# The recurrence chain of a hybrid RWKV-7 / MLA layer: one PSUM bank per head pair, the output's state product moved beside U, a full-width identity product, and the state copied on by ScalarE

## Chip, cores and metric

The kernel runs on one core of one Trainium2 chip. The metric is the device time of one execution in microseconds (us). Three executions were timed, and one more was profiled; the profile gives times in us from the start of its span.

## The reference

One decoder layer over a sequence of 1024 tokens of width 1024. A modulated RMSNorm feeds one input projection. Its columns go to two groups: an RWKV-7 recurrence (8 heads of 64) and a latent attention (8 heads). Both are gated, concatenated and mapped back by an output projection; a final RMSNorm closes. The part that matters here is the recurrence:

```python
def step(state, inp):
    r_t, w_t, k_t, v_t, kk_t, a_t = inp
    sa = jnp.einsum('bhvk,bhk->bhv', state, kk_t)
    state = (state * w_t[:, :, None, :]
             - sa[..., None] * (kk_t * a_t)[:, :, None, :]
             + v_t[..., None] * k_t[:, :, None, :])
    y = jnp.einsum('bhvk,bhk->bhv', state, r_t)
    return state, y
```

It is a serial scan over the tokens with a 64x64 state for every head. All of it is float32.

## The kernel before

**Stages.** First the modulated, normalised and transposed input is made, in two parts whose sum is the float32 value (`hTh`, `hTl`). Then comes a long stage in which the input projection, cut into tiles of 128 output columns, runs as filler of TensorE (`mm3`, lines 164 to 166: three matmuls of 128x512 for each tile and slice of the contraction), while the recurrence is prepared and carried out between these matmuls. Then the attention follows, and last the output projection.

**The recurrence in chunks.** It is done in chunks of `C` = 64 tokens. A unit is four heads (two pairs, `a` = 0, 1; the two heads of a pair, `s` = 0, 1, lie on partitions 0 to 63 and 64 to 127, `rows[s]`) over 256 tokens, that is four chunks. There are eight units: four for heads 0 to 3, then four for heads 4 to 7. `prep`, `products`, `invert`, `fetch`, `tmat`, `turn_kb` and `turn_v` make a unit's matrices beforehand: `GA` (masked products, its columns 0 to C for the chain's first step and C to 2C for the output), `TT` (the inverse of a triangular matrix), `KB` (keys, for the state's update), `rq` (decayed receptance) and `eL` (the decay over the chunk). `ST` holds for each chunk, on one half of the partitions, the values and on the other half first the incoming state and then U.

**The chain.** `chain(un, nxt)` is the serial part. For each of the four chunks `i` it has three steps, with a `yield` after each, so that other work is emitted between them:

- step 1: four products `GA` x `ST` (L694, contraction over 128 rows, 64 columns), and one copy of the result to `X` by ScalarE (L697);
- step 2: four products `TT` x `X` (L701, 64 rows, 64 columns), and two scaled copies by ScalarE which write -U into `ST` (L703, L704);
- step 3: the next state. For each pair two products with a 64x64 identity add the old state `Sv` (L709), and two products `KB` x `ST` (L712, 128 rows) add to it. ScalarE multiplies by `eL` four times into the next chunk's `ST` (L720, 64 partitions each) and two times into `Sn` (L722, 128 partitions). Then the chunk's output `Y`: for each pair two products `rq` x `Sv` (L725, 64 rows) and two products `GA` x `ST` (L728, 128 rows).

The first chunk of heads 0 to 3 and of heads 4 to 7 has no old state; the last chunk of each has no next state. In PSUM (eight banks) the tile `rc` with the three results is one bank, `Y` of a unit is another, and the tags `mm`, `rp` and `rt` have two each. `post` (L739) copies a unit's `Y` to SBUF in one copy of 128x512 and normalises it.

**What sets the order.** The loop at the end of the code goes through stages `n` = 0 to 10 and steps `j` within each. At every second `j` it resumes the chain of unit `n` - 2; at fixed `j` it calls the parts of the units that are being prepared or finished; and at each `j` it emits `RATE[n]` slices of the filler. The instructions of each engine are then put in order by a planner that goes by priority (the order of emission) and by when it reckons operands to be ready; `quick` raises the priority of the chain's ScalarE instructions by 20 places (100 in the last units). On the chip each engine runs its instructions in that order. The dependencies in PSUM are kept by the framework.

Of the kernel before, what the change touches and what calls it, by code (L numbers as in the profile page):

```python
# [17 lines left out]
F32 = mybir.dt.float32  # L18
# [9 lines left out]
P = 128  # L28
# [3 lines left out]
HALF = 512  # L32
# [3 lines left out]
C = 64  # L36
# [50 lines left out]
def hymba_kernel(ctx: ExitStack, tc: tile.TileContext, x, pos, cols, cst, winit, w_ada, b_gate, w_in, w_lora, w0,  # L87
# [157 lines left out]
    with ExitStack() as s0:  # L245
# [62 lines left out]
        for i in range(4, 8):  # L308
            load_x(i)
        ws.append(load_w(GROUP[2][0], P, st, 3, st))  # L310
        acc = [[(psM if m == 0 else psA).tile([P, HALF], F32, tag=t, name=f"acc{m}{h}", bufs=1 if m == 1 else 2)
                for h, t in enumerate(tags)] for m, tags in enumerate((("mm", "mm"), ("rc", "ry"), ("rt", "rt")))]
# [365 lines left out]
    def chain(un, nxt):  # L678
# [8 lines left out]
        ps = psA.tile([P, 3, 2, C], F32, tag="rc", name="rc", bufs=1)  # L687
        Y = un["Y"] = psA.tile([P, 8, C], F32, tag="ry", name="Y", bufs=1)
        for i in range(4):
            last = i == 3 and nxt is None  # L690
            cc = [a * 4 + i for a in range(2)]
            for a in range(2):
                for s in range(2):
                    T.matmul(ps[rows[s], 0, a, :], lhsT=GA[s][a][:, i, 0:C], rhs=ST[:, cc[a], s, :], start=True, stop=True)  # L694
            X = ch.tile([P, 2, C], F32, tag="X", name="X", bufs=2)
            with quick(un):
                A.copy(X[:], ps[:, 0])  # L697
            yield
            for a in range(2):
                for s in range(2):  # L700
                    T.matmul(ps[rows[s], 1, a, :], lhsT=TT[rows[s], cc[a], :], rhs=X[rows[s], a, :], start=True, stop=True)  # L701
            with quick(un):
                A.mul(ST[lo, i:8:4, 0, :], ps[lo, 1], -1.0)  # L703
                A.mul(ST[hi, i:8:4, 1, :], ps[hi, 1], -1.0)  # L704
            yield
            Sn = None if last else ch.tile([P, 2, C], F32, tag="S", name="S", bufs=2)
            for a in range(0 if last else 2):
                for s in range(2 if Sv else 0):
                    T.matmul(ps[rows[s], 2, a, :], lhsT=ident[rows[s], rows[s]], rhs=Sv[rows[s], a, :],  # L709
                             start=True, stop=False)  # L710
                for s in range(2):
                    T.matmul(ps[rows[s], 2, a, :], lhsT=KB[:, s, cc[a], :], rhs=ST[:, cc[a], s, :],  # L712
                             start=Sv is None, stop=True)
            if not last:

                dst, n = (ST, i + 1) if i < 3 else (nxt["ST"], 0)
                with quick(un):
                    for a in range(2):
                        for s in range(2):
                            A.mul(dst[rows[s], a * 4 + n, s, :], ps[rows[s], 2, a, :], eL[rows[s], cc[a]:cc[a] + 1])  # L720
                    for a in range(2):
                        A.mul(Sn[:, a], ps[:, 2, a], eL[:, cc[a]:cc[a] + 1])  # L722
            for a in range(2):
                for s in range(2 if Sv else 0):
                    T.matmul(Y[rows[s], cc[a], :], lhsT=rq[rows[s], cc[a], 1, :], rhs=Sv[rows[s], a, :],  # L725
                             start=True, stop=False)
                for s in range(2):
                    T.matmul(Y[rows[s], cc[a], :], lhsT=GA[s][a][:, i, C:2 * C], rhs=ST[:, cc[a], s, :],  # L728
                             start=Sv is None, stop=True)
            Sv = Sn  # L730
            if i == 3 and nxt:
                nxt["S"] = Sv
            yield

    def post(un):
# [3 lines left out]
        A.copy(ys[:], Y[:])  # L739
# [270 lines left out]

    turned, la = [], latents()
# [374 lines left out]
```

## Time and profile before

| what | value |
|---|---|
| three timed executions | 925.86, 933.34, 2558.89 us; median 933.34 us |
| the profiled execution's own time | 920.99 us |
| its span in the profile | 918.8 us, 16567 instructions |
| TensorE (PE) busy with matmuls | 835.3 us, 91% of the span |
| VectorE (DVE) busy | 575.3 us, 63% |
| ScalarE (ACT) busy | 476.5 us, 52% |
| GpSimd (POOL) busy | 296.2 us, 32% |

PE is the matmul part of TensorE and PEld its weight loads. A float32 matmul stands in the trace as two records, so that four products of a step show as "x8". A row of the timeline gives a group's start, its length, engine, line, tiles and the shape: "128*64 128x64" is contraction rows by output columns of the array, then the moving operand. The ends of matmuls are modelled and overlap with the next ones, so how long a group holds the engine is read from the start of the group to the start of the next. In the windows, PEclk is the mean of the clock that TensorE was granted, 1.00 being full speed.

### The profile page before, as it was taken

Reading aid. Unit: us, or ns where it says so; the run is one execution under the profiler, and the core shown is the slowest. Engines: PE = TensorE matmul, PEld = TensorE weight load, DVE = VectorE, ACT = ScalarE, POOL = GpSimd, SP = SyncE. Lnnn points to the kernel's source line nnn. Section 1 sums busy time; section 2 is a strip of 40 time slices with the busy share of each in tenths; the row PEclk is TensorE's granted clock in tenths of the full one; section 3 lists DMA queues with packets and bytes.
Section 4 is the critical chain, followed back from the end, with each engine's and each line's share of the span. In section 5 each row is a group of like instructions: output and inputs, shape, how many; then the busy total and the mean of one; then the engine's idle time right before and its main releaser. Section 6 shows DMA issues by size and latency. Waiting matters only on the chain.

```text
span 918.8 us, 16567 instructions
## 1 busy us (share of the span) xinstructions
PE 835.3 (91%) x5812; PEld 641.2 (70%) x5812; DVE 575.3 (63%) x1462; ACT 476.5 (52%) x1112; POOL 296.2 (32%) x351
## 2 busy tenths in 40 slices
PE   1798997999999999898899999997799998989996
PEld 0586785776777777566667767765678777868885
DVE  5795349378495654955757366247778788765443
ACT  2655332444644636346245464554778888873311
POOL 1311423131232323423133122223436454454400
PEclk9999999999999999998999999999999999999998
DMA  8764433333435324435333254157102031017233
GB/s 253 247 194 153 140 110 115 95 105 88 134 118 150 118 69 135 121 69 165 118 99 104 65 151 139 49 172 203 55 18 70 21 110 59 1 56 239 85 126 126
DMA packets 131714, 106.66 MB, mean 116 GB/s; under 512 B 40616, under 2 KB 108464, under 8 KB 131632
## 3 DMA queue, kind: packets, MB, share of 16 engines
q1 hardware_dynamic: 130672, 102.46, 37.5%
q0 software_dynamic: 960, 3.15, 1.5%
q8 instruction: 46, 0.75, 0.3%
q14 instruction: 36, 0.29, 0.1%
HBM read 76.46 MB, written 29.10 MB: 115 GB/s over the span
## 4 chain that ended last, share of the span: by engine, by line
PE 66%; DVE 13%; ACT 9%; issue 4%; DMA 4%; POOL 2%; SPq 1%; POOLq 0%; DVEq 0%; ACTq 0%
PE mm L164 10%; PE mm L165 8%; PE mm L166 8%; PE po L1160 3%; PE po L1162 3%; PE po L1161 3%; PE gps L577 3%; ACT pr L1087 2%; DVE wtmp L625 2%; DVE W L627 2%; PE tp L1098 2%; ACT PTh L1107 1%; PE rc L712 1%; PE rc L694 1%; PE Y L728 1%
## 5 line engine op out<-in xcount | busy, mean ns | idle before, releaser
L164 PE MATMUL mm<-hTh,whi 128*128 128x512 f32 (+1 forms) x384 | 167.2, 435 | 3.1 <-DVE wtmp L625 2.3
L166 PE MATMUL mm<-hTh,wlo 128*128 128x512 f32 (+1 forms) x384 | 156.9, 409 | 0.0
L165 PE MATMUL mm<-hTl,whi 128*128 128x512 f32 (+1 forms) x384 | 156.8, 408 | 0.0
L157 POOL TENSOR_TENSOR wlo<-wraw,whi 128x512 fp32r<-128x512 f32 (+1 forms) x54 | 71.4, 1323 | 233.8 <-ACT whi L156 215.4
L164 PEld LDWEIGHTS mm<-hTh,whi 128*128 128x128 f32 (+1 forms) x384 | 73.3, 191 | 24.0 <-issue 3.1
L166 PEld LDWEIGHTS mm<-hTh,wlo 128*128 128x128 f32 (+1 forms) x384 | 73.2, 191 | 17.7
L165 PEld LDWEIGHTS mm<-hTl,whi 128*128 128x128 f32 (+1 forms) x384 | 73.5, 191 | 14.6 <-issue 1.4
L1091 POOL TENSOR_SCALAR pr<-pr,sm 128x512 f32<-128x512 f32 (+2 forms) x96 | 55.6, 588 | 72.4 <-DVE sm L1088 50.2
L627 DVE TENSOR_TENSOR W<-W,wtmp 128x60 f32<-128x60 f32 (+24 forms) x248 | 71.5, 288 | 5.8 <-DVE wtmp L625 0.3
L625 DVE TENSOR_TENSOR wtmp<-W,N 128x60 f32<-128x60 f32 (+24 forms) x248 | 69.2, 279 | 5.5
L156 ACT CAST whi<-wraw 128x512 fp32r<-128x512 f32 (+1 forms) x54 | 32.7, 607 | 59.4 <-PE mm L165 36.6
L720 ACT ACTIVATE ST<-rc,eL 64x64 f32<-64x64 f32 x120 | 37.1, 309 | 46.2 <-PE rc L712 44.5
L1087 ACT ACTIVATE pr<-sp,mx,rss 128x128 f32<-128x128 f32 (+3 forms) x64 | 53.3, 834 | 14.8 <-DVE mx L1080 12.3
L1108 DVE TENSOR_TENSOR PTl<-tp,PTh 128x512 fp32r<-128x512 f32 (+2 forms) x96 | 52.2, 553 | 11.8 <-ACT PTh L1107 10.1
L1079 DVE TENSOR_REDUCE mx<-sp 128x1 f32<-128x128 f32 (+3 forms) x64 | 48.0, 750 | 11.4 <-PE sp L1073 11.1
L1160 PE MATMUL po<-wo,yh 128*128 128x512 f32 x128 | 50.3, 393 | 0.8 <-ACT od L1134 0.8
L1107 ACT CAST PTh<-tp 128x512 fp32r<-128x512 f32 (+2 forms) x96 | 44.0, 477 | 13.1 <-PE tp L1098 10.2
L1098 PE MATMUL tp<-cstt,pr 128*128 128x128 f32 x288 | 45.0, 277 | 5.9 <-POOL pr L1091 2.9
L1162 PE MATMUL po<-wo,yl 128*128 128x512 f32 x128 | 50.3, 393 | 0.0
L1161 PE MATMUL po<-wo,yh 128*128 128x512 f32 x128 | 50.3, 393 | 0.0
L1119 PE MATMUL op<-PTh,Vt 128*128 128x256 f32 (+1 forms) x160 | 42.1, 293 | 5.1 <-ACT od L1134 5.1
L584 DVE TENSOR_TENSOR GA<-gps,cstt 128x512 f32<-128x512 f32 x32 | 21.4, 684 | 29.4 <-PE Y L728 22.6
(279 smaller groups left out, 1934.0 us busy)
## 6 DMA issues: line engine op xcount, KB each, us to landing
wraw<-in_w_in SPq DMA_DIRECT2D x52, 256.0 KB, 3.1
wa<-in_w_ada SPq DMA_DIRECT2D x64, 128.0 KB, 3.1
xt<-in_x SPq DMA_DIRECT2D x8, 512.0 KB, 7.4
wg<-in_w_ada SPq DMA_DIRECT2D x32, 128.0 KB, 2.5
N<-d_n SPq DMA_DIRECT2D x32, 128.0 KB, 3.1
wor<-in_w_out SPq DMA_DIRECT2D x16, 256.0 KB, 3.1
cr<-d_c SPq DMA_DIRECT2D x14, 256.0 KB, 3.4
d_c<-craw SPq DMA_DIRECT2D x10, 256.0 KB, 2.2
```

The lines of the kernel that those rows point to most:

```text
L157: G.tensor_tensor(lo[:, :, :m], raw[:, :, :m], hi[:, :, :m].bitcast(F32), ALU.subtract)
L164: T.matmul(ps[:m], lhsT=hi[:, k % 4, :m], rhs=a, start=first, stop=False)
L165: T.matmul(ps[:m], lhsT=hi[:, k % 4, :m], rhs=b, start=False, stop=False)
L166: T.matmul(ps[:m], lhsT=lo[:, k % 4, :m], rhs=a, start=False, stop=last)
L625: V.tensor_tensor(t, W[:, 0:n, u:u + 1].to_broadcast([P, n, m]), N[:, u:u + 1, u + 1:32].to_broadcast([P, n, m]), ALU.mult)
L627: V.tensor_tensor(W[:, 0:n, u + 1:32], W[:, 0:n, u + 1:32], t, ALU.subtract)
L1087: A.activation(pr[:, 0:n], sp[:, 0:n], AF.Exp, scale=rss[:, i:i + 1], bias=mx[:], accum_out=sm[:])
L1091: G.tensor_scalar(pr[:, a:e], pr[:, a:e], sm[:], 1.0, ALU.mult, ALU.mult)
L1098: T.transpose(tp[:, j, :], pr[:, (j0 + j) * P:(j0 + j + 1) * P], ident)
L1160: T.matmul(ps, lhsT=yh[k][:, ts_], rhs=hi, start=first, stop=False)
L1161: T.matmul(ps, lhsT=yh[k][:, ts_], rhs=lo, start=False, stop=False)
L1162: T.matmul(ps, lhsT=yl[k][:, ts_], rhs=hi, start=False, stop=last)
```

## The change

It has five parts. (1) `rc` and `Y` become one tile `bank` of two banks, allocated once: pair `a` has bank `a`, with slots of 64 columns: 0 for step 1, 1 for step 2, 2 for the next state and 4 to 7 for the outputs of the four chunks. The accumulators of the first stage are spread over the tags accordingly. (2) The four products `rq` x `Sv` move from behind step 3 to right behind the products `TT` x `X` of step 2. (3) The four output products `GA` x `ST` move ahead of the state's products. (4) The four 64x64 identity products become two of 128x128, one for each pair, and they are emitted ahead of all four `KB` products. (5) ScalarE multiplies by `eL` once for each pair into `Sn`, on 128 partitions, and then copies `Sn` into the next chunk's `ST` with two copies of 64x128, in place of the four multiplications of 64x64.

```diff
-        ps = psA.tile([P, 3, 2, C], F32, tag="rc", name="rc", bufs=1)
-        Y = un["Y"] = psA.tile([P, 8, C], F32, tag="ry", name="Y", bufs=1)
+        ps = un["Y"] = bank
...
             for a in range(2):
                 for s in range(2):
-                    T.matmul(ps[rows[s], 1, a, :], lhsT=TT[rows[s], cc[a], :], rhs=X[rows[s], a, :], start=True, stop=True)
+                    T.matmul(ps[rows[s], a, 1, :], lhsT=TT[rows[s], cc[a], :], rhs=X[rows[s], a, :], start=True, stop=True)
+            for a in range(2 if Sv else 0):
+                for s in range(2):
+                    T.matmul(ps[rows[s], a, 4 + i, :], lhsT=rq[rows[s], cc[a], 1, :], rhs=Sv[rows[s], a, :],
+                             start=True, stop=False)
             with quick(un):
-                A.mul(ST[lo, i:8:4, 0, :], ps[lo, 1], -1.0)
-                A.mul(ST[hi, i:8:4, 1, :], ps[hi, 1], -1.0)
+                A.mul(ST[lo, i:8:4, 0, :], ps[lo, :, 1], -1.0)
+                A.mul(ST[hi, i:8:4, 1, :], ps[hi, :, 1], -1.0)
             yield
             Sn = None if last else ch.tile([P, 2, C], F32, tag="S", name="S", bufs=2)
+            for a in range(2):
+                for s in range(2):
+                    T.matmul(ps[rows[s], a, 4 + i, :], lhsT=GA[s][a][:, i, C:2 * C], rhs=ST[:, cc[a], s, :],
+                             start=Sv is None, stop=True)
+            for a in range(0 if last or Sv is None else 2):
+                T.matmul(ps[:, a, 2, :], lhsT=ident, rhs=Sv[:, a, :], start=True, stop=False)
             for a in range(0 if last else 2):
-                for s in range(2 if Sv else 0):
-                    T.matmul(ps[rows[s], 2, a, :], lhsT=ident[rows[s], rows[s]], rhs=Sv[rows[s], a, :],
-                             start=True, stop=False)
                 for s in range(2):
-                    T.matmul(ps[rows[s], 2, a, :], lhsT=KB[:, s, cc[a], :], rhs=ST[:, cc[a], s, :],
+                    T.matmul(ps[rows[s], a, 2, :], lhsT=KB[:, s, cc[a], :], rhs=ST[:, cc[a], s, :],
                              start=Sv is None, stop=True)
...
                 with quick(un):
                     for a in range(2):
-                        for s in range(2):
-                            A.mul(dst[rows[s], a * 4 + n, s, :], ps[rows[s], 2, a, :], eL[rows[s], cc[a]:cc[a] + 1])
-                    for a in range(2):
-                        A.mul(Sn[:, a], ps[:, 2, a], eL[:, cc[a]:cc[a] + 1])
-            for a in range(2):
-                for s in range(2 if Sv else 0):
-                    T.matmul(Y[rows[s], cc[a], :], lhsT=rq[rows[s], cc[a], 1, :], rhs=Sv[rows[s], a, :],
-                             start=True, stop=False)
-                for s in range(2):
-                    T.matmul(Y[rows[s], cc[a], :], lhsT=GA[s][a][:, i, C:2 * C], rhs=ST[:, cc[a], s, :],
-                             start=Sv is None, stop=True)
+                        A.mul(Sn[:, a], ps[:, a, 2], eL[:, cc[a]:cc[a] + 1])
+                    for s in range(2):
+                        A.copy(dst[rows[s], n:8:4, s, :], Sn[rows[s]])
...
-        A.copy(ys[:], Y[:])
+        A.copy(ys[:].rearrange("p (a i) t -> p a i t", a=2), Y[:, :, 4:8])
...
+    bank = psA.tile([P, 2, 8, C], F32, tag="rc", name="rc", bufs=1)
```

More of the change, by code (lines that the diff above doesn't have):

```diff
@@ L310, in hymba_kernel @@
         ws.append(load_w(GROUP[2][0], P, st, 3, st))
-        acc = [[(psM if m == 0 else psA).tile([P, HALF], F32, tag=t, name=f"acc{m}{h}", bufs=1 if m == 1 else 2)
-                for h, t in enumerate(tags)] for m, tags in enumerate((("mm", "mm"), ("rc", "ry"), ("rt", "rt")))]
+        acc = [[(psM if m == 0 else psA).tile([P, HALF], F32, tag="rt" if m else "mm", name=f"acc{m}{h}")
+                for h in range(2)] for m in (0, 2)]
+        both = psA.tile([P, 2, HALF], F32, tag="rc", name="acc1", bufs=1)
+        acc.insert(1, [both[:, h] for h in range(2)])
         seq = [(0, 0), (1, 0), (0, 1), (1, 1)] + [(kt, h) for kt in range(2, NK) for h in range(2)]
@@ L693, in chain @@
                 for s in range(2):
-                    T.matmul(ps[rows[s], 0, a, :], lhsT=GA[s][a][:, i, 0:C], rhs=ST[:, cc[a], s, :], start=True, stop=True)
+                    T.matmul(ps[rows[s], a, 0, :], lhsT=GA[s][a][:, i, 0:C], rhs=ST[:, cc[a], s, :], start=True, stop=True)
             X = ch.tile([P, 2, C], F32, tag="X", name="X", bufs=2)
             with quick(un):
-                A.copy(X[:], ps[:, 0])
+                A.copy(X[:], ps[:, :, 0])
             yield
```

## The prediction

> **What bounds the kernel now.** I read the page first: its totals and the chain of waits.
>
> ```profile
> span 918.8 us, 16567 instructions
> PE 835.3 (91%) x5812; PEld 641.2 (70%) x5812; DVE 575.3 (63%) x1462; ACT 476.5 (52%) x1112; POOL 296.2 (32%) x351
> PE 66%; DVE 13%; ACT 9%; issue 4%; DMA 4%; POOL 2%; SPq 1%; POOLq 0%; DVEq 0%; ACTq 0%
> ```
>
> TensorE holds two thirds of the chain that ended last. The next question is whether that is so in the part that the change touches. The instructions of single source lines (durations, then first and last start) place the chain's first and last products:
>
> ```profile
> L694 PE MATMUL rc<-ST,GA x256: 222/222/369, 176.1 to 611.2; 128*64 128x64 f32 x128
> L728 PE MATMUL Y<-ST,GA x256: 222/222/367, 182.1 to 620.1; 128*64 128x64 f32 x128
> ```
>
> So I asked for the window from 176 to 620 us, and for two short ones around one chunk's third step:
>
> ```profile
> core 0: us, PE busy (x) PEld busy (x) DVE busy (x) ACT busy (x) POOL busy (x), PEclk, DMA share, GB/s
> 176.00:620.00 444.00, 429.05 (x3580) 311.64 (x3579) 265.31 (x762) 226.98 (x579) 125.55 (x117) 0.97 0.40 114
> 309.91:313.32 3.41, 3.41 (x43) 2.81 (x43) 3.28 (x14) 2.83 (x8) 2.09 (x1) 1.00 0.45 141
> 313.32:316.73 3.41, 3.41 (x9) 2.20 (x7) 3.20 (x11) 0.62 (x1) 2.40 (x2) 0.50 0.39 108
> ```
>
> In the chain's 444 us TensorE is busy for 429.05 (97%), VectorE for 265 (60%), ScalarE for 227 (51%). So a microsecond of TensorE time taken out here is worth nearly a microsecond at the end, and ScalarE time is worth little by itself. Where TensorE does wait, the list of its waits in this window says for whom (total, times, longest):
>
> ```profile
> PE Y L725 <- ACT S L722: 2.5, 2, 1.4
> PE mm L164 <- DVE wtmp L625: 2.3, 1, 2.3
> PE Y L728 <- ACT ST L703: 1.8, 4, 0.7
> PE gps L577 <- DVE kb L555: 1.8, 2, 1.4
> PE rc L694 <- ACT S L722: 0.9, 1, 0.9
> ```
>
> The chain itself makes TensorE wait for some 5 us in 444. With 32 chunks a chunk comes round every 444 / 32 = 13.9 us, and the filler covers the serial latency. The chain is therefore no latency problem; it costs what its products hold TensorE. That is not their busy time, since records overlap, but start to start. One whole third step:
>
> ```profile
> 309.92 0.33 PE L709 MATMUL rc<-S,cstt 64*64 64x64 f32 x4
> 310.18 0.34 PE L712 MATMUL rc<-ST,KB 128*64 128x64 f32 x4
> 310.44 0.33 PE L709 MATMUL rc<-S,cstt 64*64 64x64 f32 x4
> 310.70 0.34 PE L712 MATMUL rc<-ST,KB 128*64 128x64 f32 x4
> 310.97 0.33 PE L725 MATMUL Y<-S,rq 64*64 64x64 f32 x4
> 311.23 0.34 PE L728 MATMUL Y<-ST,GA 128*64 128x64 f32 x4
> 311.50 0.33 PE L725 MATMUL Y<-S,rq 64*64 64x64 f32 x4
> 311.76 0.34 PE L728 MATMUL Y<-ST,GA 128*64 128x64 f32 x4
> 312.02 1.05 PE L509 MATMUL nps<-cstt,sq 128*128 128x2 f32 x8
> 312.94 0.49 PE L164 MATMUL mm<-hTh,whi 128*128 128x512 f32 x1
> ...
> 320.30 0.45 PE L701 MATMUL rc<-X,TT 64*64 64x64 f32 x8
> 320.68 0.65 PE L536 MATMUL kps<-cstt,sq 128*128 128x128 f32 x4
> 321.09 0.48 PE L164 MATMUL mm<-hTh,whi 128*128 128x512 f32 x1
> ```
>
> The eight groups of two products each hold TensorE from 309.92 to 312.02, 2.10 us: 0.26 for each group. The four products of step 2, in one shape, take 320.30 to 320.68, 0.38. So two products more in the same shape add 0.38 - 0.26 = 0.12, and the other 0.26 - 0.12 = 0.14 of a group comes with the change of shape. Step 3 changes shape eight times. That is the quantity this edit works on.
>
> **The change part by part.** How often each group occurs (two records a product, eight for a chunk):
>
> ```profile
> L728 PE MATMUL Y<-ST,GA 128*64 128x64 f32 x256 | 23.1, 246 | 1.8 <-ACT ST L703 1.8
> L725 PE MATMUL Y<-S,rq 64*64 64x64 f32 x240 | 21.0, 248 | 2.5 <-ACT S L722 2.5
> L712 PE MATMUL rc<-ST,KB 128*64 128x64 f32 x240 | 19.7, 245 | 0.0
> L709 PE MATMUL rc<-S,cstt 64*64 64x64 f32 x224 | 18.6, 243 | 0.4 <-ACT ST L704 0.4
> ```
>
> L709 is there in 224 / 8 = 28 chunks, L712 and L725 in 30, L728 in 32.
>
> *TensorE, removed.* 2.10 us in each of the 28 full chunks.
>
> *TensorE, added.* The `rq` products stand behind `TT` x `X` in the same 64x64 shape: two pairs at 0.12 = 0.24. `GA` x `ST`, four in one shape: 0.38. `KB` x `ST`, four in that shape too: 0.38, though behind the identities and so with a change of its own. The identity products in 128x128 have no row. Nearest is L536, two float32 products of 128x128 with 128 moving columns: 320.68 to 321.09, 0.41, of which I take all, although only 64 columns move here. From below 0.26, the time of an L709 group; from above half of L509's 0.92 for eight records, 0.46. Sum 0.24 + 0.38 + 0.41 + 0.38 = 1.41. Saved: 0.69 a chunk, 28 x 0.69 = 19.3 us. In the two last chunks (no next state) four groups, 1.05, become 0.24 + 0.38: 0.43 each, 0.9 together. The two first chunks have one shape in step 3 before and after: nothing. **Together -20.2 us.** The bounds: identity at 0.26 gives -24.4, at 0.46 -18.8; and if the planner puts filler between `TT` and `rq` in all 30 chunks, each pays a change of shape more, 30 x 0.14 = 4.2, which leaves -14.6 with the dear identity.
>
> [...]
>
> *ScalarE.* The rows of the same chunk, and of the copies:
>
> ```profile
> 311.09 1.29 ACT L720 ACTIVATE ST<-rc,eL 64x64 f32<-64x64 f32 x4
> 312.40 0.52 ACT L722 ACTIVATE S<-rc,eL 128x64 f32<-128x64 f32 x2
> ...
> L704 ACT ACTIVATE ST<-rc 64x128 f32<-64x128 f32 x32 | 8.7, 273 | 0.7
> L739 ACT COPY ys<-Y 128x512 f32<-128x512 f32 x8 | 4.7, 584 | 4.9 <-PE Y L728 4.9
> ...
> 421.51 0.27 PE L709 MATMUL rc<-S,cstt 64*64 64x64 f32 x2 [0.36 <-ACT ST L704]
> ```
>
> Six instructions in 1.29 + 0.52 = 1.81 us become two multiplications (0.52, the L722 row) and two copies of 64x128 (0.27 each by the L704 row): 1.06. That is 0.75 x 30 = 22 us off ScalarE, which is 51% busy here, so it counts nothing directly. But the multiplications start only at 311.09, behind the last `KB` product, though the first pair was ready at 310.44; and at 421.51 the identity, which reads no `ST`, waited for ScalarE's L704. Both show that users of one bank wait for each other. So the next step 1 waits for all six today, for the four in future, and the first of them need not wait for the other pair. The waits `L694 <- S` (0.9) and `L725 <- S` (2.5, since `rq` then uses a state that is a chunk old) go: -3.4 us.
>
> *New waits.* With outputs and chain in one bank, L703 waits for the `rq` products too (0.24) and `GA` x `ST` for both of L703 and L704 (0.27 more). Queued behind L703 on ScalarE are evacuations of the filler, behind `GA` on TensorE the identities, `KB` and filler. In the four places where TensorE waits for L703 now that is 4 x 0.51 = 2.0 us; elsewhere filler stands between. The copy of `Y` (0.58, L739) must now fit between step 1 and step 2 of the next unit; behind it on ScalarE stand the filler's evacuations, and step 2 on TensorE waits for it. A chunk is six steps `j`, so the two `j` between are some 13.9 / 3 = 4.6 us, most of it filler, and I take nothing; uncovered it would cost 8 x 0.58 = 4.7. The first stage's accumulators and the DMAs stay as they were: no queue has a transfer moved past it.
>
> *Clock.* After the window 309.91 to 313.32, filled with step 3 and L509, the clock is 0.50 for the next 3.41 us. Over the stage 0.97 means 3% of 444 = 13 us lost. Denser steps should bring fewer such dips; I take a third, -4 us.
>
> *Given back.* The other 20 groups of waits do not shrink: VectorE's 265 us have to fit into a shorter stage. The two rows of waits for VectorE hold 4.1 us. I take +3 for their growth, between 0 and all of the gain.
>
> Sum: -20.2 - 3.4 + 2.0 - 4 + 3 = -22.6 us against the profiled execution: span 918.8 to 896.2, and its own time, 2.2 longer, 920.99 to 898.4. The median of the runs shown is 12.35 above the profiled execution, so I forecast 933.34 - 22.6, about **911 us**.
>
> **Rivals.**
>
> *The clock stays up.* The low clock follows the sparse third step; from 2.10 to 1.17 us (0.38 + 0.41 + 0.38) it may fall below what brings the dip about, and the 13 us come back whole instead of 4. Then 902 us. For it: the dip behind 313.32. [...]
>
> *Given back elsewhere.* The order is planned, and a shorter chain changes what stands where on five engines. VectorE waits in this stage already reach TensorE (2.3 and 1.8 us in single rows). If half to all of the 20.2 is lost to waits for VectorE, or the planner tears the groups apart (-14.6 instead of -20.2), the result is 918 to 933, about 925. That is also how it looks if the change does not do what it says. Against: VectorE is 60% busy.
>
> *Slower: the chain becomes the bound, at the copies.* The next step 1 now hangs on a multiplication and a copy behind it, both in ScalarE's one queue. If other activations slip between (0.58 us for one of 128x512, by the L739 row) and TensorE's fixed order has step 1 next, it stands. It decides when such a stall is longer than the 0.69 us saved, in most chunks: with two of them, 1.16 us in all 30, it is +35 - 20 = +15, so 948 us. Against: 13.9 us a chunk, and the chain of today waits for ScalarE in single places only.
>
> **How the numbers follow.** Forecast 0.52 (its own range 903 to 918), clock 0.14 (902), given back 0.25 (925), slower 0.09 (948). About 2% is what a measurement of this kernel tells from no change; 2% faster is 914.7. All of the clock rival and most of the forecast lie below it (0.14 + 0.43), the rest of the forecast and the given-back case within it (0.09 + 0.25). The range leaves out the slower case and the outer end of the clock's: 896 (cheap identity and full clock together would be 898) to 932.
>
> **What would show it.** In the profile after: TensorE's step 3 as three groups, `GA` x8, identity x4, `KB` x8, in about 1.17 us, and `rq` x8 right behind `TT` x8, 0.62 together. The identity's group start to start tells 0.26, 0.41 or 0.46. ScalarE has four instructions in 1.06 us. PEclk over the stage above 0.97 speaks for the clock rival; more waits of TensorE for VectorE's W, wtmp and kb for the given-back case; waits of step 1 for the new copies for the slower one. The prediction is wrong if the groups shrink as said and the stage doesn't.

## The result and the profile after

The change made the kernel slower: 941.27 us (median of four executions, 935.87 to 943.54) against 932.91 us, 0.9% by the medians; the ratio on record is 1.0141 with a 95% interval of 1.0091 to 1.0190. That is clear of noise by its interval, though less than the 2% that the prediction took as its mark. The forecast was 911 us, its range 896 to 932. The profiled execution took 942.0 us. All ratios leave out executions more than 1.5% above the fastest of their kernel, while medians are of all executions. The page of the changed kernel, totals and chain:

```profile
span 940.0 us, 16270 instructions
PE 840.6 (89%) x5700; PEld 653.2 (69%) x5700; DVE 582.9 (62%) x1462; ACT 458.6 (49%) x1052; POOL 298.7 (32%) x351
PE 55%; DVE 19%; ACT 10%; issue 5%; POOL 5%; DMA 4%; SPq 1%; POOLq 0%; DVEq 0%; ACTq 0%
```

TensorE's share of the chain fell from 66% to 55%, VectorE's rose from 13% to 19%. To see where the time sits I cut both traces at the same two events, the chain's first product and the attention's first score. The window of before, then that of the changed kernel:

```profile
176.10:648.40 472.30, 450.08 (x3671) 326.95 (x3671) 285.56 (x800) 241.44 (x605) 136.63 (x130) 0.97 0.42 118
```

```profile
179.60:669.30 489.70, 450.35 (x3560) 334.70 (x3560) 290.02 (x801) 223.35 (x545) 140.13 (x130) 0.94 0.40 114
```

The stage is 17.4 us longer (472.3 to 489.7). TensorE without a matmul: 22.2 us before, 39.3 after, +17.1. The clock: 30.7 us of the stage ran at 0.50 before, 61.8 after; at half speed half of that is lost, 15.4 and 30.9, +15.5 (a filler matmul of 128x512 takes 0.23 us start to start at full clock, 327.25 to 327.48 in the changed kernel, and 0.43 at half, 440.59 to 441.02 in before). What is left of the length is work at full clock, 434.8 before and 419.5 after: **-15.3**. So the change did take work off TensorE, some three quarters of what was promised, and in this pair of executions the stage gave back twice as much, half as idle time and half as low clock. (TensorE was also idle for 2.4 us of the time at half clock before and for 5.2 after, which this sum counts twice; counted once, work fell by 13.9 us and the clock took 14.1.)

**How typical is this pair?** It overstates the loss: the two profiled executions are 21.0 us apart, the medians 8.4. The profiled execution of before is the fastest of that kernel on record, and TensorE was granted 0.973 of full speed over its span. In 76 other executions of before, on the four chips of the experiments, the granted clock was 0.947 to 0.972, median 0.963, and the median time 930.0 us. The four executions of the changed kernel had 0.949 to 0.953, median 0.951. Time multiplied by clock gives an estimate of the time at full clock: 930.0 x 0.963 = 896 us before and 941.3 x 0.951 = 895 us after. By this estimate typical executions of the two kernels are equally long at full clock, so idle time has used up the saved work, and the kernel became slower through the clock: 0.012 x 935 = 11 us.

A third step and its step 2 in the changed kernel, from the timeline:

```profile
325.68 0.45 PE L702 MATMUL rc<-X,TT 64*64 64x64 f32 x8
325.96 0.40 PE L705 MATMUL rc<-S,rq 64*64 64x64 f32 x8
326.29 0.66 PE L538 MATMUL kps<-cstt,sq 128*128 128x128 f32 x4
...
329.61 0.45 PE L714 MATMUL rc<-ST,GA 128*64 128x64 f32 x8
329.99 0.66 PE L717 MATMUL rc<-S,cstt 128*128 128x64 f32 x4
330.58 0.45 PE L720 MATMUL rc<-ST,KB 128*64 128x64 f32 x8
330.96 0.50 PE L164 MATMUL mm<-hTh,whi 128*128 128x512 f32 x1
```

Start to start: `TT` and `rq` 0.61 together, `GA` 0.38, the two wide identities 0.59, `KB` 0.38. Step 3 holds TensorE for 1.35 us, not the 1.17 forecast. Saved per full chunk: 2.10 - 1.35 - 0.24 = 0.51, and 28 x 0.51 + 0.9 = 15.2, close to the 15.3 (or 13.9) us that the stage shows.

TensorE's waits in the window 176 to 660 (total, times, longest):

```profile
PE gps L579 <- DVE wtmp L627: 10.3, 4, 3.9
PE ytps L767 <- POOL ys L761: 4.0, 4, 1.4
PE gps L579 <- DVE GA L586: 4.0, 1, 4.0
PE rc L714 <- ACT ST L709: 3.8, 5, 1.3
PE rc L695 <- ACT ST L729: 2.8, 3, 1.1
```

The new waits are at L579, the masked products of the next unit, which need `kb`, `rq` and `kn` from VectorE: 14.3 us. In before three rows of this kind held 4.6 us: the 1.8 that the prediction shows, and these two of the same list:

```profile
PE gps L577 <- DVE wtmp L625: 1.6, 2, 1.2
PE gps L577 <- DVE kb L554: 1.2, 1, 1.2
```

The second row of the changed kernel is new: the transposition of the finished outputs waits for the normalised `ys`.

One of the stalls, in the timeline of TensorE and VectorE:

```profile
328.99 1.32 DVE L629 TENSOR_TENSOR W<-W,wtmp 128x68 f32<-128x68 f32 x1
...
331.53 0.40 PE L166 MATMUL mm<-hTh,wlo 128*128 128x512 f32 x1
...
332.42 0.47 DVE L541 SCALAR_TENSOR_TENSOR kn<-k,colt,kps 128x256 f32<-128x256 f32 x1
...
333.47 0.69 DVE L554 TENSOR_TENSOR rq<-kn,E 128x512 f32<-128x512 f32 x1
...
334.99 0.68 DVE L556 TENSOR_TENSOR kb<-kn,Ei 64x512 f32<-64x512 f32 x1
335.60 0.21 DVE L627 TENSOR_TENSOR wtmp<-W,N 128x66 f32<-128x66 f32 x1
335.82 2.90 PE L579 MATMUL gps<-rq,kb 64*128 64x128 f32 x16 [3.90 <-DVE wtmp L627]
```

The list names `wtmp`, an inversion step of another unit, because it is VectorE's last event before the products start; what they need stands just ahead of it: `kb` ends at 335.67. So the products wait for VectorE's queue, in which the preparation of this unit stands between inversion steps. The windows of 3.41 us around it (columns as in the prediction):

```profile
327.55:330.96 3.41, 3.41 (x30) 2.59 (x28) 3.24 (x6) 0.00 (x0) 2.57 (x2) 1.00 0.25 74
330.96:334.38 3.42, 0.97 (x7) 0.49 (x3) 3.35 (x13) 1.11 (x4) 0.11 (x1) 1.00 0.25 82
334.38:337.79 3.41, 1.97 (x13) 2.00 (x14) 3.21 (x10) 0.00 (x0) 0.00 (x0) 0.51 0.35 93
337.79:341.21 3.42, 3.42 (x19) 2.33 (x17) 2.56 (x10) 0.82 (x3) 0.00 (x0) 0.50 0.10 14
...
344.62:348.03 3.41, 3.41 (x10) 2.83 (x10) 1.70 (x10) 0.00 (x0) 0.00 (x0) 0.50 0.02 5
348.03:351.45 3.42, 3.42 (x19) 2.23 (x18) 0.00 (x0) 1.16 (x3) 1.30 (x1) 0.99 0.26 38
```

VectorE, 60% busy over the stage, is full here (3.24, 3.35 and 3.21 of 3.41). And the clock: TensorE is busy for 0.97 in the second window, and the next four run at half clock, 13.7 us, though TensorE is busy for 12.3 of them. At half clock half of these 12.3 us is lost, so by this estimate the wait of 3.9 us came with some 6 us more. The waits of 3.4 and 4.0 us that end at 404.13 and 520.20 each have 10.2 us of low clock with them, which begin at 402.69 and 518.74, within the wait. These three are the only stalls of TensorE over 3 us in this stage; the longest in the stage of before has 2.3 us. Of the shorter ones some are followed by low clock and some are not: 1.7 us up to 213.71 by 6.8 us of it from 214.96 on, 2.2 us up to 659.79 by full clock until 668.90 (1.00). The stretches at half clock in the two stages last 3.41, 6.83, 10.24 or 13.65 us. Work did not end this one at once: TensorE was busy all through 337.79 to 341.21, and the clock came back only at 348.03, two windows later.

The last finding concerns the copy of the outputs, L739. One unit's end, from the timeline:

```profile
287.75 0.45 PE L714 MATMUL rc<-ST,GA 128*64 128x64 f32 x8
...
300.50 0.33 PE L695 MATMUL rc<-ST,GA 128*64 128x64 f32 x2
302.40 0.45 PE L695 MATMUL rc<-ST,GA 128*64 128x64 f32 x6
...
303.05 0.59 ACT L739 COPY ys<-rc 128x512 f32<-128x512 f32 x1
304.71 1.04 POOL L753 TENSOR_TENSOR ys<-ys,s 128x512 f32<-128x512 f32 x1 [6.01 <-DVE s L752]
...
310.48 1.06 PE L767 MATMUL ytps<-cstt,ys 128*64 128x128 f32 x8 [0.59 <-POOL ys L761]
```

The last output product starts at 287.75, the copy only at 303.05, behind the next unit's step 1 in the same banks. In the first five units it starts 9.1 to 14.8 us after the output is complete; in before it was 0 to 1.8. The normalisation behind it, on VectorE and GpSimd, moves with it.

### The profile page after: what moved, and what is told of

It reads as the page before. It is cut to its first block, busy times and chain, and to the rows that moved or that the text cites. A ratio compares the mean times of both kernels' runs of the same rounds, so it can differ in the third digit from the quotient of the medians.

```text
span 940.0 us, 16270 instructions
## 1 busy us (share of the span) xinstructions
PE 840.6 (89%) x5700; PEld 653.2 (69%) x5700; DVE 582.9 (62%) x1462; ACT 458.6 (49%) x1052; POOL 298.7 (32%) x351
## 4 chain that ended last, share of the span: by engine, by line
PE 55%; DVE 19%; ACT 10%; issue 5%; POOL 5%; DMA 4%; SPq 1%; POOLq 0%; DVEq 0%; ACTq 0%
PE mm L164 8%; PE mm L166 7%; PE mm L165 7%; DVE W L629 4%; PE gps L579 3%; PE po L1162 3%; PE po L1164 3%; PE po L1163 3%; DVE wtmp L627 3%; ACT pr L1089 2%; PE tp L1100 2%; ACT PTh L1109 2%; DMA wg<-in_w_ada 1%; PE lps L365 1%; PE op L1121 1%
## 5 line engine op out<-in xcount | busy, mean ns | idle before, releaser
L164 PE MATMUL mm<-hTh,whi 128*128 128x512 f32 (+1 forms) x384 | 169.8, 442 | 3.1 <-DVE wtmp L627 2.1
L166 PE MATMUL mm<-hTh,wlo 128*128 128x512 f32 (+1 forms) x384 | 158.8, 414 | 0.0
L629 DVE TENSOR_TENSOR W<-W,wtmp 128x60 f32<-128x60 f32 (+24 forms) x248 | 76.4, 308 | 5.8 <-DVE wtmp L627 0.3
L579 PE MATMUL gps<-rq,kb 64*128 64x128 f32 x256 | 32.8, 336 | 21.5 <-DVE wtmp L627 10.3
L579 PEld LDWEIGHTS gps<-rq,kb 64*128 64x128 f32 x256 | 27.6, 226 | 29.5 <-issue 20.5
```

Source lines behind the costliest of these rows:

```text
L164: T.matmul(ps[:m], lhsT=hi[:, k % 4, :m], rhs=a, start=first, stop=False)
L166: T.matmul(ps[:m], lhsT=lo[:, k % 4, :m], rhs=a, start=False, stop=last)
L579: T.matmul(pp[s][:, i, :], lhsT=kb[rows, c, :, :].rearrange("p a t -> p (a t)"), rhs=rq[rows, c, :, :].rearrange("p a t -> p (a t)"), star ...
L629: V.tensor_tensor(W[:, 0:n, u + 1:32], W[:, 0:n, u + 1:32], t, ALU.subtract)
```

## The experiments

All times are medians with the ratio to before on the same chip; "clock" is the median of the clock granted over each execution. The last four columns are of the one profiled execution, between the same two events as above: length, TensorE idle, time at half clock, and work (length less idle less half of the time at half clock). Time at half clock differs between executions of one kernel, so for the clock the column of medians is the better guide.

| run | us | ratio, 95% | clock | length | idle | half clock | work |
|---|---|---|---|---|---|---|---|
| before | 932.9 | | 0.963 | 472.3 | 22.2 | 30.7 | 435 |
| changed | 941.3 | 1.0141 [1.0091, 1.0190] | 0.951 | 489.7 | 39.3 | 61.8 | 420 |
| e1 | 940.8 | 1.0109 [1.0049, 1.0170] | 0.953 | 490.0 | 39.0 | 61.9 | 420 |
| e2 | 929.2 | 0.9915 [0.9868, 0.9963] | 0.960 | 478.5 | 23.9 | 44.5 | 432 |
| e3 | 935.1 | 1.0054 [1.0021, 1.0086] | 0.952 | 486.3 | 39.5 | 62.1 | 416 |
| e4 | 946.4 | 1.0179 [1.0123, 1.0235] | 0.943 | 497.4 | 40.9 | 73.3 | 420 |
| e5 | 909.7 | 0.9794 [0.9740, 0.9848] | 0.960 | 465.0 | 27.2 | 51.2 | 412 |
| e6 | 907.7 | 0.9778 [0.9709, 0.9848] | 0.972 | 464.7 | 20.2 | 30.7 | 429 |
| e7 | 962.9 | 1.0364 [1.0307, 1.0420] | 0.947 | 514.5 | 39.0 | 81.9 | 435 |
| e8 | 939.9 | 1.0118 [1.0056, 1.0181] | 0.949 | 485.7 | 36.0 | 58.4 | 421 |
| e9 | 940.1 | 1.0099 [1.0054, 1.0143] | 0.945 | | | | |
| e10 | 926.0 | 0.9913 [0.9870, 0.9957] | 0.956 | 475.8 | 30.6 | 55.2 | 418 |
| e11 | 933.7 | 1.0043 [1.0008, 1.0079] | 0.950 | 486.1 | 31.9 | 68.7 | 420 |
| e12 | 927.9 | 1.0008 [0.9974, 1.0042] | 0.960 | 472.9 | 31.1 | 41.6 | 421 |
| e13 | 934.0 | 1.0048 [1.0011, 1.0084] | 0.963 | 491.8 | 34.1 | 61.4 | 427 |
| e14 | 927.3 | 0.9959 [0.9915, 1.0004] | 0.962 | 475.7 | 29.8 | 38.2 | 427 |
| e15 | 887.7 | 0.9506 [0.9432, 0.9581] | 0.974 | 448.6 | 24.0 | 28.1 | 411 |
| e16 | 922.3 | 0.9848 [0.9767, 0.9929] | 0.961 | 476.3 | 29.6 | 62.8 | 415 |

The column of work is the plainest result: wherever the products are grouped by shape it is 12 to 19 us lower than in its counterpart, whatever the time does (e13 and e14 hold some 9 us of added matmuls). The clock of before in the first row is that of the 76 executions above. (e9's profiled execution took 949.5 us, 9 above its median, so its stage is not in the table.)

**Is it the place of the preparation?** e1 (on the changed kernel) and e2 (on before) call a unit's preparation two `j` earlier:

```diff
-(9, 9, 10, 11, 12, 14, 14)
+(7, 7, 8, 9, 10, 12, 12)
```

> The changed kernel with the preparation of units 2 to 6 called two steps j earlier (7, 7, 8, 9, 10, 12, 12 instead of 9, 9, 10, 11, 12, 14, 14); its products stay where they are. Theory A (TensorE did get shorter by some 15 us, but its queue reaches the products L579 before VectorE has written kb; it stands, and the idle stretch halves the clock): the waits of L579 for VectorE fall from 14 us to under 6, the granted clock over the chain's stage rises from 0.94 to 0.96 or more, and the time falls by 12 to 25 us, below the kernel before. Rival B (the chain itself is slower, through the shared banks and the copies): the time stays within 5 us. Rival C (the clock falls in any order of the work): L579 waits less, but the granted clock stays at 0.94 and the time falls by no more than 6 us.

> The kernel before with the same earlier preparation, as the control. Theory A: the kernel before waits little for VectorE at its products (some 4 us in units 2 to 6, clock 0.97), so it gains at most 5 us or is moved by the planner's new order within 8 us either way; the changed kernel with the same edit is then faster than this one by 8 to 20 us. Rival B: this one stays faster than the changed kernel with the same edit. Rival C: both stay as far apart as they were, some 13 us.

e1's waits:

```profile
PE ytps L767 <- POOL ys L761: 6.7, 5, 2.8
PE y1ps L655 <- DVE T L646: 4.7, 4, 2.8
PE rc L714 <- ACT ST L709: 4.2, 5, 1.3
PE gps L579 <- DVE GA L586: 3.3, 3, 1.3
...
PE gps L579 <- DVE wtmp L627: 1.5, 1, 1.5
PE gps L579 <- DVE W L629: 1.5, 1, 1.5
PE gps L579 <- DVE kb L557: 1.0, 3, 0.4
```

The waits at L579 fell from 14.3 to 7.3 us and the time did not move: `ytps` went from 4.0 to 6.7, the inversion's products came in (4.7), and TensorE's idle time stayed at 39 us. So the waits moved to other places, and theory A's gain of 12 us or more did not come. Before itself gains 0.85% from the same move by the ratio, and nothing by the medians (929.2 against 929.4 on its chip).

**Each part by itself.** e3 goes back to 64x64 identities, e4 to ScalarE's six multiplications, e8 puts the `rq` products back into step 3. e7 keeps of the change only the two banks with the outputs in them: order of the products, identities and ScalarE's part are those of before.

```diff
 # e3
-                T.matmul(ps[:, a, 2, :], lhsT=ident, rhs=Sv[:, a, :], start=True, stop=False)
+                for s in range(2):
+                    T.matmul(ps[rows[s], a, 2, :], lhsT=ident[rows[s], rows[s]], rhs=Sv[rows[s], a, :], start=True, stop=False)
 # e4
+                        for s in range(2):
+                            A.mul(dst[rows[s], a * 4 + n, s, :], ps[rows[s], a, 2, :], eL[rows[s], cc[a]:cc[a] + 1])
...
-                    for s in range(2):
-                        A.copy(dst[rows[s], n:8:4, s, :], Sn[rows[s]])
```

> The changed kernel with the four 64x64 identity products back (still ahead of KB, all four together). The wide identity held TensorE for 0.59 us in the trace, the four small ones should hold 0.38 (0.26 and one pair more, 0.12): 28 times 0.21, 6 us less on TensorE. Theory A: the time falls by less than these 6 us, or not at all, since what TensorE saves it waits for at the products. Rival B and C: the time falls by about 6 us.

> The changed kernel with ScalarE's part undone: four multiplications of 64x64 from PSUM into ST and two into Sn, 1.81 us instead of 1.11 (two multiplications, two copies). Theory A: no effect of its own, within 8 us either way by the planner's order. Rival B in the form that the copies hold the chain: the waits of step 1 for ScalarE (2.8 us after, 0.9 before) go and the time falls by more than 8 us.

> The changed kernel with the rq products back in step 3, ahead of GA x ST, the rest as changed. TensorE then has a change of shape more in each of 30 chunks, some 0.14 us, 4 us in all. Theory A: the time rises by no more than these 4 us and may fall, within 8 us either way. Rival B in the form that the multiplications L708 waiting for rq hold the chain: the waits of L714 for L709 (3.8 us) go, and the time falls by 5 us or more in spite of the dearer order.

> The kernel before with part 1 of the change alone: a bank per pair with the outputs in the same banks; products, their order and ScalarE's instructions as before. Theory A: TensorE's groups hold it as long as before (2.10 us a chunk), so nothing reaches the products earlier; the time stays within 8 us of the kernel before. Rival B: the shared banks make the chain wait (output copies, the two scaled copies), TensorE's waits for ScalarE in the chain's stage rise from 5 us to over 10, and the time rises by 8 to 15 us, most of what the whole change costs.

e3's third step in the timeline:

```profile
325.13 0.45 PE L714 MATMUL rc<-ST,GA 128*64 128x64 f32 x8
325.51 0.45 PE L718 MATMUL rc<-S,cstt 64*64 64x64 f32 x8
325.89 0.45 PE L721 MATMUL rc<-ST,KB 128*64 128x64 f32 x8
```

Four narrow identities hold TensorE for 0.38, two wide ones for 0.59: the wide product costs 28 x 0.21 = 5.9 us of work, and the ratio falls from 1.0141 to 1.0054, the median by 6.1 us. That is what rivals B and C said: these 6 us of TensorE did arrive at the end. ScalarE's part is not the loss: without it the kernel is no faster (1.0179 against 1.0141; the intervals overlap). Nor is the place of `rq` (1.0118). In the order of before, the shared banks alone cost 3.6%, 33 us, at unchanged work, more than twice what either theory allowed. e7's waits:

```profile
PE rc L726 <- ACT S L723: 5.5, 6, 2.6
PE ytps L768 <- POOL ys L762: 3.9, 4, 1.5
PE gps L579 <- DVE wtmp L627: 3.6, 3, 2.6
```

The first row is the order of before in shared banks: `rq` x `Sv` writes an output into the bank that ScalarE is still reading the state from (5.5 us in six waits for L723, the longest 2.6). Before has 2.5 us of the same wait with the banks apart, so not all of the row is the sharing. The changed order removes that row; the second and third rows remain in the changed kernel. How much of the 33 us is left in the changed order e7 does not show. The nearest pair in a grouped order is e3 (shared banks) and e12 below (separate banks, the products grouped a little otherwise), 1.0054 and 1.0008, so some 4 us.

**Is it VectorE's load?** e5 (changed) and e6 (before) run 16 of the 31 steps of the triangular inversion and leave the rest out.

```diff
-for u in range(31):
+for u in range(16):
```

> The changed kernel with the second half of the triangular inversion left out (16 of its 31 steps on VectorE; the matrix TT is then not the inverse, only the time is read): it takes the work away that makes VectorE late for the products. Theory A (TensorE waits for VectorE at the products, and these waits bring the low clock): the waits of L579 fall from 14 us to under 5, the granted clock over the chain's stage rises from 0.94 to 0.96 or more, the time falls by 15 to 30 us, and it is then below the kernel before with the same cut. Rival B (the chain itself, through banks and copies): it falls by no more than the kernel before with the same cut, and stays some 12 us above that.

> The kernel before with the same half of the inversion left out (TT is not the inverse, only the time is read). Theory A: it waits less for VectorE to begin with, so it gains 3 to 12 us only, and ends 5 to 15 us above the changed kernel with this cut. Rival B: it ends some 12 us below it.

With 44 to 46 us less on VectorE in the stage both became faster, the changed kernel by 3.4% and before by 2.2%, and they end level: 909.65 and 907.68 us. The waits of L579 fall to 3.8 us in e5, as theory A said, but e5 does not end below e6, as it said too. The changed kernel's handicap is gone, but of its 17 us less of work nothing is left at the end. By the table it went into 7 us more of idle time and 20.5 us more at half clock, worth 10; the median clocks, 0.960 against 0.972, say the same (0.012 x 909 = 11 us). VectorE's load is one cause, then, not the only one.

**Is it the late copy?** e9 emits the copy of the outputs at the end of the unit's last chunk, ahead of the next unit's step 1; e10 has the narrow identities besides.

```diff
+            if i == 3:
+                ys = un["ys"] = evp.tile([P, 8, C], F32, tag="p2", name="ys", bufs=2)
+                A.copy(ys[:].rearrange("p (a i) t -> p a i t", a=2), ps[:, :, 4:8])
```

> The changed kernel with one instruction moved: ScalarE's copy of a unit's outputs to SBUF (L739) is emitted at the end of the unit's last chunk, ahead of the next unit's step 1, instead of one step j behind it. In the changed kernel this copy starts 9 to 15 us after the last output product in units 0 to 4, because it shares the banks with the next step 1 (0 to 2 us before the change). Theory D (the shared banks tie the output copy to the next unit; the normalisation behind it moves 10 us back into the next preparation on VectorE and GpSimd, and TensorE waits for both): the copy starts within 3 us, the waits of ytps for GpSimd (4.0 us) go, those of the products L579 fall from 14 us to under 8, and the time falls by 12 to 25 us, to 916 to 929. Theory A (VectorE is late only because TensorE got shorter): the copy is early but the time falls by less than 5 us. Rival B in the form of the chain's own waits (L714 for L709, L695 for L729, 6.6 us): they stay, and so does the time, within 5 us.

> The same with the four 64x64 identity products instead of the two wide ones, 6 us less of TensorE. Theory D: 4 to 8 us below the kernel with the early copy and wide identities, 910 to 924. Theory A: within 3 us of it.

In e9 the copy does start early, 0 to 1.4 us after the last output in the first five units, and the row `ytps` for `ys` is gone. Yet theory D missed: 1.0099, no different from the changed kernel. e10 came out at 0.9913, a median of 926.0, just above theory D's 924. Against e3 (1.0054), which has the same identities and the late copy, the early copy is worth 1.4%, 13 us, by the ratios and 9 to 10 us by the medians. Between e9 and e10 the clock differs most: times the median clock, e9 is 888 us and the changed kernel 895, e10 885 and e3 890. So by this estimate the early copy saved 5 to 7 us at full clock in both cases; in e9 the clock fell from 0.951 to 0.945, in e10 it rose from 0.952 to 0.956. What moved the clock is open; each edit makes the planner order all engines anew. In e10 the row `ytps` for `ys` is gone too, and 9.5 us of the products' waits stay (15.0 in e3):

```profile
PE gps L579 <- DVE wtmp L627: 5.1, 2, 3.1
PE gps L579 <- DVE W L629: 4.4, 2, 3.3
```

**The saving without shared banks.** e11 has the banks and ScalarE's part of before and orders the products in groups of one shape: step 2's `TT` with the identity and `rq` of pair 0, then `KB` and `GA` of pair 0, identity and `rq` of pair 1, `KB` and `GA` of pair 1. e12 adds the change's ScalarE part.

> The kernel before, with its two separate banks and its ScalarE instructions, but its products put together by shape: identity and rq of pair 0 beside step 2, then KB and GA of pair 0, identity and rq of pair 1, KB and GA of pair 1. A chunk then has three changes of shape in step 3 instead of eight: 0.24 + 3 times 0.38 = 1.38 us instead of 2.10, 28 times 0.72 and some more, 20 us less of TensorE, with no bank shared. Theory D: most of it is seen, the time falls by 8 to 20 us against the kernel before, to 910 to 922. Theory A: TensorE only gets to its waits for VectorE sooner; the time stays within 6 us of the kernel before.

> The same with ScalarE's part of the change too (two multiplications into Sn, two copies into ST). Theory D and A: within 5 us of the run without it; if step 1's waits for ScalarE count, 2 to 5 us below.

e11's waits, and its stage:

```profile
PE gps L577 <- DVE wtmp L625: 9.3, 3, 3.7
...
PE gps L577 <- DVE W L627: 1.8, 1, 1.8
```

```profile
176.60:662.70 486.10, 454.18 (x3671) 332.02 (x3671) 287.18 (x801) 239.99 (x605) 138.89 (x130) 0.93 0.41 115
```

The work falls by 15 us, as much as in the changed kernel, and the time does not fall (1.0043 in e11, as theory A said, and 1.0008 in e12). In e11 there are 11 us of waits for VectorE at the same products and 68.7 us at half clock. (Its time multiplied by its clock is 887 us, against 896 before, so by this estimate some of the saving is there at full clock, and the lower clock takes it.) This is the clearest evidence against my step "a microsecond of TensorE is a microsecond at the end": the shared banks are not needed for the gain to vanish.

**Does the low clock follow the stalls?** e13 puts dense dummy matmuls (6 for units 2 and 3, 14 for units 4 and 5, about 9 us of added work) ahead of the products at L579, so that TensorE is busy while it waits. e14 is the same on e10.

```diff
+        for _ in range({2: 6, 3: 6, 4: 14, 5: 14}.get(un["n"], 0) if q == 0 else 0):
+            T.matmul(pp[0][:].rearrange("p a t -> p (a t)"), lhsT=hTh[0][:, 0:P], rhs=hTh[1][:, 0:HALF], start=True, stop=True)
```

> The changed kernel with dummy matmuls of 128x512 in front of the first products of units 2 to 5 (6, 6, 14 and 14 of them, into the products' own PSUM tile, which the products then overwrite): 1.4 and 3.2 us of dense work in the places where TensorE stood 1.7, 1.3, 3.9 and 3.4 us for VectorE. Theory E (the low clock comes from TensorE standing still): the waits of L579 in these units shrink to under 1 us, the five stretches of low clock there (37 of 62 us at half clock) shrink to under 15, and the time falls by 8 to 15 us although 9 us of work are added. Theory C (the low clock comes in any case): the granted clock stays at 0.94 over the stage and the time stays or rises by up to 9 us.

> The same dummy matmuls in the kernel with the early output copy and 64x64 identities (926 us, where TensorE stood 1.9, 1.1, 3.1 and 3.3 us). Theory E: time at half clock over the stage falls from 55 to under 35 us, the time to 912 to 920. Theory C: 926 to 935.

e13 took 934.0 us, ratio 1.0048 against 1.0141: faster by 7 to 9 us with 9 us of work added, and no stall over 1.1 us is left at these products in units 2 to 5. In the profiled execution the total at half clock did not fall (61.4 us against 61.8): the stretches at these products went and others came, behind `ytps` (5.0 us of waits) among them. But that execution, 941.7 us at a clock of 0.954, is not typical of e13. The median clock of its ten executions is 0.963, that of before, against 0.951 in the changed kernel: 0.012 x 934 = 11 us. This speaks for theory E: filling the stalls brought the clock back. In e14 the time at half clock fell nearly as far as theory E asked (55.2 to 38.2, for under 35) and the median clock rose from 0.956 to 0.962, worth 6 us; with 9 us of work added the time stayed (0.9959 against 0.9913), which is theory C's time.

**Both causes taken away.** e15 is e10 with the inversion cut as in e5 and e6; e16 is e10 with the early preparation of e1.

> The kernel with the early output copy and 64x64 identities, and with the second half of the inversion left out (TT is not the inverse, only the time is read): neither the late copy nor VectorE's lateness is left. If the two together ate the gain, it ends 8 to 18 us below the kernel before with the same cut (907.7), at 890 to 900. If TensorE's saving is lost for another reason, it stays within 5 us of 907.7.

> The kernel with the early output copy and 64x64 identities, with the preparation of units 2 to 6 called two steps j earlier. With the late copy this moved the waits from the products to the normalisation and to tmat and gained nothing. If the late copy was what stood in its way, it now falls by 6 to 15 us to 911 to 920; if VectorE's order is the limit in any case, it stays within 6 us of 926.

The stage of e6, then that of e15:

```profile
170.70:635.40 464.70, 444.53 (x3653) 324.04 (x3653) 241.23 (x590) 241.14 (x604) 140.90 (x131) 0.97 0.42 120
```

```profile
171.00:619.60 448.60, 424.63 (x3653) 313.02 (x3653) 241.07 (x591) 221.48 (x544) 138.62 (x131) 0.97 0.45 125
```

887.65 us against e6's 907.68 (on two chips; by the ratios, 0.9506 to 0.9778, it is 2.7%), with the same cut on both sides and the same clock. TensorE's busy time falls by 20 us, the stage of the profiled executions by 16, the median by 20: for once the end follows. Neither edit alone shows this (e5 against e6: +2 us; e10 against before on its chip: -4 by the medians, -8 by the ratio). So the expected gain exists, and it came whole only with both the early copy with narrow identities and room on VectorE; copy and identities were not separated under that cut. e16, which computes everything, has the lowest ratio of the complete versions: 0.9848 [0.9767, 0.9929]; by the medians, 922.26 against 932.89 on its chip, it is 1.1% below before. The intervals of e2 and e10 overlap with it, so it is not shown to be the fastest. It lies just above the 911 to 920 expected if the late copy had stood in the way and within 6 us of 926, which was the expectation for VectorE's order as the limit; its largest wait is again for VectorE, at the inversion's products (5.7 us).

## Why the prediction was wrong, step by step

- **"A microsecond of TensorE time taken out here is worth nearly a microsecond at the end"** is the step that failed. TensorE's 97% was a mean over the stage. In before VectorE is busy for 3.35 to 3.41 us of the 3.41 ahead of each wait at the masked products, and there TensorE already waited 4.6 us. With less TensorE work between these places it arrived there earlier and waited longer: 14.3 us in the changed kernel, 11.1 in e11. The sign was there: of the waits for VectorE I showed two rows, 4.1 us, and left out the 1.6 and 1.2 at the masked products and a row of 0.5, so the list held 7.4 us for VectorE, 4.6 of it at this one line. With VectorE relieved alone (e5 against e6) the step still fails, by idle time and by the clock; with VectorE relieved, the copy early and the identities narrow (e15) it holds. For the 6 us of e3 it held as well, so it is no rule that every microsecond is lost.
- **TensorE's work**: mechanism right, one term mis-sized. `TT` with `rq` took 0.61 (0.62 forecast), `GA` and `KB` 0.38 each as forecast, the wide identities 0.59 in place of 0.41 and above the upper bound of 0.46. The row I took, L536, was followed by a matmul of its own shape, so its 0.41 has no change of shape behind it. Work fell by 15.3 us (13.9 when idle time at half clock is counted once), not 20.2.
- **"The copy of `Y` ... I take nothing"**: a term put at nothing that was not nothing. I priced the copy's own 0.58 us against the gap between two steps of the chain. What mattered was its time of start, 9 to 15 us late, which moved the normalisation on VectorE and GpSimd towards the time when the next unit's preparation was due. Its size is not settled: e10 against e3 says 9 to 13 us, e9 against the changed kernel nothing in time and some 7 us at full clock. e7 against before (+33 us, outputs in the chain's banks with nothing else of the change) holds it together with the wait of `rq` for the state, which the changed order avoids.
- **Waits that go, new waits (-3.4, +2.0)**: the rows of L725 and L694 for `S` went as said; L714 for `ST` (3.8) and L695 for the copy (2.8) came. Together 6.6 us against 5.2, so +1.4 where I had -1.4.
- **Clock (-4)**: wrong in sign. One part went as I had expected: the stretches right behind windows filled by the chain's own small products fell from five (23.8 us) to two (6.8). But five stretches in the stage, 44.4 us, now stand behind windows in which TensorE was idle for 1.7 to 2.6 of 3.41 us, where before had one of 3.4. I had counted sparse steps and left out idle time. That denser steps bring fewer dips was my estimate; no run shows it. What the runs show is a window in which TensorE was busy for 3.41 of 3.41 us and half clock behind it (313.32), and more half clock, 61.8 us against 30.7, in the kernel whose steps are denser and whose idle time is longer. I had also read the clock from an execution with 0.973; over all executions the median is 0.963 before and 0.951 after, some 11 us lost where I took 4 gained.
- **Given back (+3)**: idle time rose by 17.1 us, more than the work that was saved, and 31.1 us more at half clock come on top. The rival with this mechanism had 0.25; its end, 933 us, allowed only for losing the gain. It had no term for the clock, and the result lies beyond it.
- **Slower at the copies (948)**: the sign was right, the mechanism not. Waits of step 1 for ScalarE's copies are 2.8 us in all, and e4, without these copies, is no faster.
- **What would show it**: "more waits of TensorE for VectorE's W, wtmp and kb", and "the groups shrink as said and the stage doesn't". Both happened.

What stays open: what the late copy costs by itself, and why the clock fell in e9 and rose in e10. The share of the clock, some 11 us, is an estimate from the recorded clocks, and that filling the stalls brings it back rests on e13 with e14 half for it. The planner orders five engines anew for every edit, and single slow stretches move with it.

## What to carry to other kernels

A busy share of 97% does not price a saving where another engine is full for a while: look at short windows around the places where the engine already waits, however briefly, because here the faster engine waited longer exactly there (14.3 us at the masked products, 4.6 before). Compare the granted clocks of all executions before reading a pair of profiles; the pair here showed more than twice the difference of the medians. When a result shares a bank with a serial chain, see where its copy is emitted: emitted behind the chain's next step it came 9 to 15 us late, ahead of it 0 to 1.4. For small products, group those of one shape of tile before widening them: here the two wide ones took longer, 0.59 us against 0.38 for four narrow ones.

## What the hardware showed that I had not expected

- Two 128x128 identities with 64 moving columns between 128x64 groups hold TensorE for 0.59 us; four 64x64 ones in the same place 0.38.
- One stall of 3.9 us came with 13.7 us at half clock, of which only the first 3.4 us had idle time in them; the other two stalls over 3 us in the changed kernel's stage, of 3.4 and 4.0 us, with 10.2 us each.
- An inversion step on VectorE of 128x68 took 1.32 us (328.99, shown above) while GpSimd ran an operation of 128x512. In the changed kernel the steps of 128x60 to 128x75 during which GpSimd ran nothing took 0.21 to 0.24. No run took GpSimd's work away, so what made the step long was not shown.
